# A decoder step of sparse attention and mLSTM: five hand-out times, two spacings, two orders

## The chip, the cores and the metric

The kernel runs on one core of one Trainium2 chip. The metric is device time in microseconds (us) for one execution of the whole step, given as the median of some runs. Five engines have queues of their own and run at the same time: TensorE (PE, matrix products), VectorE (DVE), ScalarE (ACT), GpSimd (POOL) and SyncE (SP). Transfers (DMAs) are started by instructions in the queue of an engine, here mostly SP, POOL and ACT.

## The reference, cut to what matters

One layer works on a prompt of 1024 tokens and on 8 decode tokens with 4096 cached positions each; together they are 1032 columns. In short:

```python
p = project(rmsnorm(x, norm_w), w_in, b_i, b_f)    # 14 column groups of one projection
# DSA heads, for each query:
s = einsum(relu(einsum(q_idx, k_idx)), w_idx) * IDX_SCALE      # 16 index heads of 64
_, idx = top_k(where(key_pos <= pos, s, -inf), 256)            # index search
att = softmax(q @ k[idx] * ATT_SCALE) @ v[idx]                 # 8 heads, 2 kv heads, 128 wide
# mLSTM heads, 4 of them: recurrence over the prompt with states C, n, m; one step for decode
h = num / maximum(abs(den), exp(-m_t))
a  = att * silu(z_att)
mo = rmsnorm(h) * ml_norm_w * sigmoid(o) * silu(z_ml)
y  = rmsnorm(x + concatenate([a, mo]) @ w_out) * final_norm_w
```

Outputs are y for prompt and decode, and the new k, v, index keys and mLSTM states. Everything is fp32. The decode tokens do the same search over their paged caches, and gather the 256 selected rows of k and v.

## The kernel before, in words

**Projection in tiles.** The 61 tiles of 128 output columns of w_in are worked off in program order; a tile is the unit in which all time is planned. fp32 products are made from a rounded high part (H) and the rest (L) of each operand: three matmuls, H·H, H·L and L·H. Tiles 0 to 20 (`proj`, L1591) hold the index queries and keys, k, v and q of attention. From tile `T_G` = 21 on `gate_stage()` works the other 40 tiles (mLSTM q, k, v, its gates o and z, and the gate of attention) as 20 column pairs of a Strassen-Winograd 2x2 form: 7 products for each pair, so 140 products of 48 matmuls (128x258, L1778). Stage 1 makes two of the seven for all pairs (products 0 to 39), stages 2, 3 and 4 one each (40 to 59, 60 to 79, 80 to 99), stage 5 the last two (100 to 139).

**Partial sums.** Between the stages a pair's partial sums lie in DRAM, in `spD`. `get` (L1795 to L1799) loads one, `combine` (L1874, on DVE) adds the product out of PE's banks, `put` (L1802) stores it. In stages 2 to 4 `ask(x, i)` calls `get` for pair i two products ahead; i = 0 and 1 are asked for before the stage. `get` stands in `issue_after(pace["put"])`: its load comes behind the last `put` store in SP's order. The partial goes into one of a few ring tiles (named `ev`, `rstd`, `xH` or `xL` in the rows, since these tiles reuse older memory). Weights come by L1763 on SP, their sums (`usD`) from POOL; the input's halves come by L1731 (`xL<-xsD`), and ACT (L1766) and DVE (L1767) split what has to be split.

**The jobs beside it.** Attention, index search and mLSTM are written as generators and handed out between the matmuls. A `Job(name, start, end, weight, gen, conditions)` stands in a `Lane`; lanes run their jobs one after the other. At each quarter tile the lane takes pieces up to a `yield`; a piece of weight w is charged w times the quarters left until `end`, over the weight that is left. So `end` and the number of yields set how densely a job is handed out. Lane 0 has gates, index (index scores L482 to L487 and search), att (attention of the prompt) and ml (mLSTM of the prompt). Lane 1 has prep, dscore and dsel (decode search), qrows (puts the decode queries into rows, L1287 and L992, and stores them as `qrowS`, L995), datt (decode attention; loads the rows back to all partitions, `qb`, L1305) and dml. Lane 2 makes the weight sums. att waits until datt is done; datt goes on only when index is done and tile 33.8 has been reached.

At the end of dsel SP stores the selected rows' numbers (`slotS<-rai`, L1186) and loads them in another layout (`idxs<-slotS`, L1187), one directly behind the other. att loads v blocks (`pP<-avS`, L603) and transposes them (L611). ml loads decay rows (`rb<-rowS`, L851) and q, k, v (L854), makes scores and transposes (L873 to L878), exponents on ACT, and products (L909, L915); its outputs go to `hS` (L948).

**The end.** The output projection begins with its last 264 columns (L2086) and goes on with the first 768 in Strassen form (L2153). Its input, the gated branch outputs, comes from loads of gate and branch on POOL (L1557, L1561), a product on DVE (L1568, L1569), the high part on ACT (L1576) and the low part on DVE (L1577). Weights come from SP as `wraw` (L265) and are split on ACT (L268) and DVE (L269).

A scheduler puts each engine's instructions into one fixed order when the program is built. `high_priority`, `pin` and `issue_after` steer it; adds that are listed in `late` are placed later with the rows that use them.

Of the kernel before, what the change touches and what calls it, by code (L numbers as in the profile page):

```python
# [42 lines left out]
T_AK = 9  # L43
T_AV = 11
T_AQ = 13
T_G = 21
# [131 lines left out]
def body(tc, A, stop=None):  # L178
# [27 lines left out]
    early = ExitStack()  # L206
# [15 lines left out]
    pace = {}  # L222
# [608 lines left out]
    def job_ml():  # L831
        gT = mlc["gT"]
        with tc.tile_pool(name="ml", bufs=2) as pm:
# [115 lines left out]

            steps = [(c, h0) for c in range(8) for h0 in (0, 2)]  # L950
            ld = [load(*steps[0])]
            for _ in range(3):
                yield 1
            ld.append(load(*steps[1]))
            yield 1
# [328 lines left out]
    def job_qrows():  # L1284
        with tc.tile_pool(name="qr", bufs=1, side="right") as pd:
            qc = pd.tile([128, NB, 8], F32, name="qc")
            V.tensor_copy(qc, dec[:, T_AQ:T_AQ + 8, :].rearrange("p j b -> p b j"))  # L1287
            yield 1
            rows(pd, qc.rearrange("p b j -> p (b j)"), qrowS, "jk")
            yield 1  # L1290

# [232 lines left out]
    def ix_weight(blocks):  # L1524
# [4 lines left out]
    groups = ((2, 3), (4, 5), (6, 7))  # L1529

    lanes = [Lane([Job("gates", 5, T_AK - 0.5, 14500, job_gates),
                   Job("index", T_AK + 1.5, 31.5, 6000 + sum(map(ix_weight, groups)), lambda: job_index(groups)),
                   Job("att", T_G + 18.2, 48.0, 2 * 2 * sum(2 * (1 + (i + 1) * 0.5) for i in range(8)) + 24, job_att, att_free),
                   Job("ml", T_G + 20, 56.4, 39, job_ml, lo_done)]),
             Lane([Job("prep", 3, T_AK + 1.8, 1 + 16 * 2, job_prep),
                   Job("dscore", T_AK + 2.4, 17.9, 56 + 128 + 2, job_dscore),
                   Job("dsel", T_AK, 27.2, 4000 + 31 * 1700 + 12000 + 16 * 2800 + 2000, job_dsel),
                   Job("qrows", T_G + 0.2, 28, 2, job_qrows),
                   Job("datt", T_G + 12.1, 38.0, 10000 + 8 * 8000 + 15000 + 5 * 2500 + 8000 + 8000 + 5000, job_datt),
                   Job("dml", T_G + 20, 55.5, 28000 + 16 * 2500 + 5000, job_dml, hi_done)]),  # L1540
             Lane([Job("sums", T_AK + 2.5, 33.0, 4 * NP + 2 * NS, job_usum)])]
# [132 lines left out]
    def gate_stage():  # L1674
# [22 lines left out]
        def ev():  # L1697
            return take("ev", outs)
# [92 lines left out]
        def flat(e):  # L1791
            return e.rearrange("p c t -> p (c t)")

        def get(x, i, e=None):
            with tc.high_priority():  # L1795
                e = ev() if e is None else e
                with tc.issue_after(pace["put"]):
                    SY.dma_start(flat(e), spD[x, i])
            return e  # L1799

# [83 lines left out]
        for i in range(0, NP, 2):  # L1884
# [4 lines left out]
            for y in range(2):  # L1889
                product(6, i + y, 2, both[y], False)  # L1890
                with tc.high_priority():
                    if X0[i + y][0] == "mk":
                        e = ev()
                        for c in range(2):
                            V.scalar_tensor_tensor(e[:, c], both[y][c], MK_SCALE, rs[:, c], OP.mult, OP.mult)
                    else:
                        e = combine(both[y], rs, OP.mult, ev())
# [13 lines left out]
        got = []  # L1911

        def ask(x, i):
            got.append(get(x, i))

        def asker(x, i):
            return (lambda: ask(x, i)) if i < NP else None
# [3 lines left out]
        for i in range(NP):  # L1921
            ps = two()
# [7 lines left out]
        for i in range(NP):  # L1930
            ps = two()
# [15 lines left out]
        for i in range(NP):  # L1947
            ps = two()
# [36 lines left out]
        for p, (z, i, y) in enumerate(order):  # L1985
# [9 lines left out]
            e, g = fetched.pop(p)  # L1995
# [121 lines left out]
    HB = NBK // 2  # L2117
    pt = ctx.enter_context(tc.tile_pool(name="pt", bufs=1, side="right"))
    ss = pt.tile([128, NBK, 8], F32, name="ss")
    yt = [[None] * 4 for _ in range(NBK)]  # L2120
# [86 lines left out]
    late = []  # L2207
# [31 lines left out]
    for n in range(2):  # L2239
        ps = banks3(n)  # L2240
# [29 lines left out]
    def add(y, p, x, op=OP.add):  # L2270
        return lambda: pin(V.tensor_tensor(y, p, x, op))  # L2271
# [6 lines left out]
    for n in range(2):  # L2278
        ps = banks3(n)
        for k in range(8):  # L2280
            with tc.high_priority():
                T_ = tsplit(wblock(1, n, k, *single(n, k)), None, n > 0)
            blocks(ps, k, sP2[k], T_, LOW)
            spread(2)
            j = 4 + k // 2 if n else k
            if k % 2 if n else k < 4:
                pairprep(j)
                if j < 5:
                    with tc.high_priority():
                        pairsub(j)  # L2290
        for b in LOW:
            late.append(add(yt[b][n], ps[b], yt[b + HB * n][n]))
        if not n:
            rows3(square, LOW, 0)
    spread(9)
# [58 lines left out]
    for n in range(2):  # L2354
        ps = banks3(n)
# [18 lines left out]
    for n in range(2):  # L2374
        ps = banks3(n)
# [26 lines left out]
    ps = banks3(0)  # L2402
# [10 lines left out]
    ps = banks3(1)  # L2413
# [83 lines left out]
```

## Time and profile before

| | |
|---|---|
| median of 3 runs | 1942.56 us (1938.98 to 1945.68) |
| the profiled execution | 1935.76 us |
| its span | 1934.0 us |
| PE busy | 1886.7 us, 98% |
| DVE busy | 1393.2 us, 72% |
| ACT busy | 913.9 us, 47% |
| POOL busy | 512.7 us, 27% |
| mean granted PE clock | 0.988 |

The span is the profiled execution from its first instruction to its last. Busy shares are means over the whole span. PE is busy nearly all of it; what it loses is read from the list of its waits, each with the line that waited and what released it, and from the granted clock in the stretch behind a wait. Times of rows count from the start of the span. A tile name in a row may be a reused one.

### The profile page before, as it was taken

The numbers are of one execution on the slowest core, as the hardware profiler recorded it, in microseconds if no ns is written. First come the engines' busy times: TensorE is split into PE (matmuls) and PEld (weight loads), VectorE is DVE, ScalarE is ACT, GpSimd is POOL, SyncE is SP. The second block draws the span as 40 slices with busy tenths as digits, with TensorE's granted clock in tenths as the row PEclk, the third lists the DMA queues.
The fourth block names the chain that finished last, engine by engine and source line by source line (L and its number), as shares of the span: only waits on it lengthen the run. The fifth ranks groups of instructions, "written<-read, shape, count | busy, mean of one in ns | idle before, by whom it ended". The sixth has DMA issues, their size and how long they took to land. (4 is left out here: it accounts for less than half of the span.)

```text
span 1934.0 us, 37287 instructions
## 1 busy us (share of the span) xinstructions
PE 1886.7 (98%) x13422; PEld 1817.4 (94%) x13422; DVE 1393.2 (72%) x3266; ACT 913.9 (47%) x1822; POOL 512.7 (27%) x600
## 2 busy tenths in 40 slices
PE   9999999999999999899999999999999989999997
PEld 9999999999999999899989999988999989987886
DVE  8554577467698886799655666547888866788776
ACT  8222254145534457532244564545566544454654
POOL 0699843320011001015211011001211341105541
PEclk9999999999999999999999999998999999999999
DMA  7577857666899778769986898556999968899797
GB/s 262 162 235 215 256 181 218 192 164 172 237 290 253 209 191 213 247 211 333 301 221 162 228 261 203 155 185 218 317 305 305 246 185 286 265 328 318 257 218 234
DMA packets 253701, 456.62 MB, mean 236 GB/s; under 512 B 38165, under 2 KB 113877, under 8 KB 249837
## 3 DMA queue, kind: packets, MB, share of 16 engines
q1 hardware_dynamic: 192445, 331.24, 52.5%
q0 software_dynamic: 27648, 102.34, 23.2%
q10 hardware_dynamic: 33424, 20.68, 3.6%
q8 instruction: 105, 1.72, 0.4%
q14 instruction: 79, 0.65, 0.1%
HBM read 363.72 MB, written 138.67 MB: 260 GB/s over the span
## 5 line engine op out<-in xcount | busy, mean ns | idle before, releaser
L1778 PE MATMUL pj<-xH 128*128 128x258 f32 x1920 | 547.9, 286 | 7.1 <-DVE rstd L1874 5.1
L1778 PE MATMUL pj<-xL,xH 128*128 128x258 f32 x1920 | 547.2, 285 | 0.0
L1778 PE MATMUL pj<-xH,xL 128*128 128x258 f32 x1920 | 546.4, 285 | 0.0
L1778 PEld LDWEIGHTS pj<-xH 128*128 128x128 f32 x1920 | 365.1, 190 | 9.8 <-DVE rstd L1874 5.3
L1778 PEld LDWEIGHTS pj<-xH,xL 128*128 128x128 f32 x1920 | 365.3, 190 | 1.7
L1778 PEld LDWEIGHTS pj<-xL,xH 128*128 128x128 f32 x1920 | 365.2, 190 | 1.6
L1591 PE MATMUL pj<-xH,wH 128*128 128x344 f32 (+1 forms) x816 | 264.8, 327 | 1.6 <-ACT xH L325 1.0
L1591 PE MATMUL pj<-xL,wH 128*128 128x344 f32 (+1 forms) x816 | 264.5, 324 | 0.1
L1591 PE MATMUL pj<-xH,wL 128*128 128x344 f32 (+1 forms) x816 | 264.5, 324 | 0.0
L269 DVE TENSOR_TENSOR wL<-wraw,wH 128x512 fp32r<-128x512 f32 (+2 forms) x151 | 118.8, 798 | 108.8 <-ACT wH L268 107.0
L268 ACT CAST wH<-wraw 128x512 fp32r<-128x512 f32 (+2 forms) x151 | 90.2, 608 | 204.8 <-PE pj L1591 130.0
L1591 PEld LDWEIGHTS pj<-xH,wH 128*128 128x128 f32 x816 | 153.2, 188 | 3.5 <-ACT xH L325 1.9
L1591 PEld LDWEIGHTS pj<-xL,wH 128*128 128x128 f32 x816 | 153.3, 188 | 0.6 <-DVE xL L326 0.3
L1591 PEld LDWEIGHTS pj<-xH,wL 128*128 128x128 f32 x816 | 153.3, 188 | 0.1
L1766 ACT CAST xH<-wH 128x1024 fp32r<-128x1024 f32 (+1 forms) x91 | 76.1, 836 | 131.0 <-PE pj L1778 73.3
L2153 PE MATMUL pj<-wH,sH 128*128 128x512 f32 x336 | 131.7, 392 | 4.1 <-DVE yt L2271 2.7
L2153 PE MATMUL pj<-wH,sL 128*128 128x512 f32 x336 | 131.5, 391 | 0.0
L1766 ACT CAST xH<-wL 128x1024 fp32r<-128x1024 f32 x91 | 76.1, 837 | 107.8 <-PE pj L1778 67.9
L2153 PE MATMUL pj<-wL,sH 128*128 128x512 f32 x336 | 123.2, 391 | 0.1
L484 ACT ACTIVATE rl<-bank 128x512 f32<-128x512 f32 (+2 forms) x160 | 79.1, 522 | 88.1 <-PE bank L482 45.5
L487 DVE SCALAR_TENSOR_TENSOR s<-rl,wiN,s 128x512 f32<-128x512 f32 (+2 forms) x150 | 106.6, 731 | 17.4 <-ACT rl L484 14.3
L1767 DVE TENSOR_TENSOR xL<-wH,xH 128x1024 fp32r<-128x1024 f32 (+1 forms) x91 | 87.1, 957 | 29.6 <-ACT xH L1766 29.3
(500 smaller groups left out, 4450.1 us busy)
## 6 DMA issues: line engine op xcount, KB each, us to landing
wraw<-in_wt_dram SPq DMA_DIRECT2D x144, 256.0 KB
usD<-in_wa_dram POOLq DMA_DIRECT2D x46, 512.0 KB, 7.8
wraw<-in_wa_dram SPq DMA_DIRECT2D x78, 256.0 KB
wraw<-in_wo_dram SPq DMA_DIRECT2D x64, 256.0 KB
usD<-in_wa_dram SPq DMA_DIRECT2D x26, 512.0 KB
wH<-in_wa_dram SPq DMA_DIRECT2D x25, 512.0 KB
wL<-in_wa_dram SPq DMA_DIRECT2D x24, 512.0 KB
spD<-ev SPq DMA_DIRECT2D x46, 258.0 KB
```

What stands on the lines that cost most here:

```text
L268: a = paced("act", SC.copy(H[:, s, :cols], raw[:, s, :cols]))
L269: return a, V.tensor_tensor(L[:, s, :cols], raw[:, s, :cols], H[:, s, :cols].bitcast(F32), OP.subtract)
L484: SC.activation(r[:, :cn], p[:, :cn], AF.Relu)
L487: v = V.scalar_tensor_tensor(s[:, c0:c0 + cn], r[:, :cn], wv, s[:, c0:c0 + cn], OP.mult, OP.add)
L1591: m = PE.matmul(ps[:cols, :cn], w_[:, k, :cols], x_[kk][:, c0:c0 + cn], start=(kk == ends[0] and z == 0), stop=(kk == ends[1] and z == 2))
L1766: paced("act", SC.copy(H[:, q], r))
L1767: paced("dve", V.tensor_tensor(L[:, q], r, H[:, q].bitcast(F32), OP.subtract))
L1778: PE.matmul(ps[c], w_[:, q, ks], x[y][:, c * CS:c * CS + CS], start=(first and q == 0 and k == 0 and z == 0), stop=(q == 1 and k == 3 and ...
L2153: PE.matmul(ps[b], S_[x][:, b * 128:b * 128 + 128], T_[y], start=(k == 0 and z == 0), stop=(k == 7 and z == 2))
```

## The change

Seven edits. Three ends in the table of jobs come sooner (index 31.5 to 28.2 tiles, att 48.0 to 47.3, ml 56.4 to 55.8), and att may start at tile 38.8 instead of 39.2. qrows ends later (28 to 29.4), and four yields instead of one stand between its copy `qc` and its rows. ml has five yields instead of three between its first and its second load. `get` has a new argument, and `ask` sets it for i = 0 and 1: those loads are no longer placed behind the last store of a partial. In the output projection, the adds of the second half of the columns are issued at once with high priority, and no longer put on the list `late`; the operands are the same. The diff:

```diff
--- before.py
+++ after.py
@@ -949,7 +949,7 @@
 
             steps = [(c, h0) for c in range(8) for h0 in (0, 2)]
             ld = [load(*steps[0])]
-            for _ in range(3):
+            for _ in range(5):
                 yield 1
             ld.append(load(*steps[1]))
             yield 1
@@ -1285,7 +1285,8 @@
         with tc.tile_pool(name="qr", bufs=1, side="right") as pd:
             qc = pd.tile([128, NB, 8], F32, name="qc")
             V.tensor_copy(qc, dec[:, T_AQ:T_AQ + 8, :].rearrange("p j b -> p b j"))
-            yield 1
+            for _ in range(4):
+                yield 1
             rows(pd, qc.rearrange("p b j -> p (b j)"), qrowS, "jk")
             yield 1
 
@@ -1529,13 +1530,13 @@
     groups = ((2, 3), (4, 5), (6, 7))
 
     lanes = [Lane([Job("gates", 5, T_AK - 0.5, 14500, job_gates),
-                   Job("index", T_AK + 1.5, 31.5, 6000 + sum(map(ix_weight, groups)), lambda: job_index(groups)),
-                   Job("att", T_G + 18.2, 48.0, 2 * 2 * sum(2 * (1 + (i + 1) * 0.5) for i in range(8)) + 24, job_att, att_free),
-                   Job("ml", T_G + 20, 56.4, 39, job_ml, lo_done)]),
+                   Job("index", T_AK + 1.5, 28.2, 6000 + sum(map(ix_weight, groups)), lambda: job_index(groups)),
+                   Job("att", T_G + 17.8, 47.3, 2 * 2 * sum(2 * (1 + (i + 1) * 0.5) for i in range(8)) + 24, job_att, att_free),
+                   Job("ml", T_G + 20, 55.8, 41, job_ml, lo_done)]),
              Lane([Job("prep", 3, T_AK + 1.8, 1 + 16 * 2, job_prep),
                    Job("dscore", T_AK + 2.4, 17.9, 56 + 128 + 2, job_dscore),
                    Job("dsel", T_AK, 27.2, 4000 + 31 * 1700 + 12000 + 16 * 2800 + 2000, job_dsel),
-                   Job("qrows", T_G + 0.2, 28, 2, job_qrows),
+                   Job("qrows", T_G + 0.2, 29.4, 5, job_qrows),
                    Job("datt", T_G + 12.1, 38.0, 10000 + 8 * 8000 + 15000 + 5 * 2500 + 8000 + 8000 + 5000, job_datt),
                    Job("dml", T_G + 20, 55.5, 28000 + 16 * 2500 + 5000, job_dml, hi_done)]),
              Lane([Job("sums", T_AK + 2.5, 33.0, 4 * NP + 2 * NS, job_usum)])]
@@ -1791,10 +1792,12 @@
         def flat(e):
             return e.rearrange("p c t -> p (c t)")
 
-        def get(x, i, e=None):
+        def get(x, i, e=None, early=False):
             with tc.high_priority():
                 e = ev() if e is None else e
-                with tc.issue_after(pace["put"]):
+                with ExitStack() as es:
+                    if not early:
+                        es.enter_context(tc.issue_after(pace["put"]))
                     SY.dma_start(flat(e), spD[x, i])
             return e
 
@@ -1911,7 +1914,7 @@
         got = []
 
         def ask(x, i):
-            got.append(get(x, i))
+            got.append(get(x, i, early=i < 2))
 
         def asker(x, i):
             return (lambda: ask(x, i)) if i < NP else None
@@ -2289,7 +2292,11 @@
                     with tc.high_priority():
                         pairsub(j)
         for b in LOW:
-            late.append(add(yt[b][n], ps[b], yt[b + HB * n][n]))
+            if n:
+                with tc.high_priority():
+                    add(yt[b][n], ps[b], yt[b + HB][n])()
+            else:
+                late.append(add(yt[b][n], ps[b], yt[b][n]))
         if not n:
             rows3(square, LOW, 0)
     spread(9)
```

The change moves instructions. Below are three places, with rows as the built program has them (line, operation, output and inputs, size); the line numbers of the changed kernel are up to 7 higher.

**SP, from the end of stage 1 on.** `rstd` is the tile that receives stage 2's first partial. Before:

```order
L1186 DMA slotS<-rai 128x16
L1187 DMA idxs<-slotS 128x16x1
L1802 DMA spD<-ev 128x516
L1731 DMA xL<-xsD 128x516
L1763 DMA wH<-usD 128x1024
L995 DMA qrowS<-jk 64x128
L1731 DMA xL<-xsD 128x516
L1802 DMA spD<-ev 128x516
L1798 DMA rstd<-spD 128x516
L1798 DMA ev<-spD 128x516
L1305 DMA qb<-qrowS 128x1024 x3
```

With the change:

```order
L1801 DMA rstd<-spD 128x516
L1764 DMA wH<-usD 128x1024
L1186 DMA slotS<-rai 128x16
L1187 DMA idxs<-slotS 128x16x1
L1805 DMA spD<-rstd 128x516
L1801 DMA ev<-spD 128x516
L1764 DMA wL<-usD 128x1024
L1732 DMA xL<-xsD 128x516
L995 DMA qrowS<-jk 64x128
L1764 DMA wH<-usD 128x512
L1805 DMA spD<-rstd 128x516
L1801 DMA ev<-spD 128x516
```

The load of the first partial stood behind the pair slotS and idxs and is now ahead of it. The three loads `qb` stood directly behind the first two loads of partials, while the low half of `rstd` was loaded five rows after them; now they stand two rows after the piece shown. Of the two halves of `rstd`, the other one is loaded far sooner, in the middle of stage 1. The pair slotS and idxs has moved by four weight loads (L1763, now L1764).

**PE, where ml begins.** `bank` is ml's output bank, `pj` that of the gate products. Before:

```order
L1778 MATMUL pj_5281<-xL,xH 128x258
L1778 MATMUL pj_5281<-xH,xL 128x258
L873 MATMUL bank<-qkv 128x128 x2
L875 MATMUL bank<-cst,qkv 128x128 x2
L878 MATMUL bank<-cst,qkv 128x128 x4
L909 MATMUL bank<-aH,dH 128x258
L915 MATMUL bank<-aH,ksH 128x258
L909 MATMUL bank<-aH,dH 128x258
```

With the change (48 matmuls of L1779 stand between the two pieces):

```order
L1779 MATMUL pj_5374<-xH 128x258
L1779 MATMUL pj_5374<-xL,xH 128x258
L1779 MATMUL pj_5374<-xH,xL 128x258
L873 MATMUL bank<-qkv 128x128 x2
L875 MATMUL bank<-cst,qkv 128x128 x2
L878 MATMUL bank<-cst,qkv 128x128 x4
L1779 MATMUL pj_5375<-xH 128x258
```

```order
L1779 MATMUL pj_5376<-xL,xH 128x258
L1779 MATMUL pj_5376<-xH,xL 128x258
L909 MATMUL bank<-aH,dH 128x258
L915 MATMUL bank<-aH,ksH 128x258
L909 MATMUL bank<-aH,dH 128x258
L915 MATMUL bank<-aH,ksH 128x258
```

The products L909 stood directly behind L873 to L878. Now a product of the gate stage stands between them. L873 itself is 4.5 products (of 48 matmuls) nearer to the program's start than it was, the first load of `rb` on SP 7 weight loads.

**DVE, where the gate stage ends.** `mx` and `mL` belong to the input of the output projection (L1569 and L1577, now L1570 and L1578), L1874 (now L1877) is the combine. Before, behind the last combine:

```order
L1577 TENSOR_TENSOR mL_18608<-mx,mH_18607 128x264
L1829 SCALAR_TENSOR_TENSOR rstd<-rstd 128x516
L1830 SCALAR_TENSOR_TENSOR rstd<-xL,rstd 128x516
L1829 SCALAR_TENSOR_TENSOR ev<-ev 128x516
L1830 SCALAR_TENSOR_TENSOR ev<-xL,ev 128x516
L300 MEMSET rr 128x16
L1569 SCALAR_TENSOR_TENSOR mx<-mH_18793,nw,mL_18794 128x264
L1577 TENSOR_TENSOR mL_18794<-mx,mH_18793 128x264
L269 TENSOR_TENSOR wL<-wraw,wH 128x512 x3
L1569 SCALAR_TENSOR_TENSOR mx<-mH_18858,nw,mL_18859 128x264
L1577 TENSOR_TENSOR mL_18859<-mx,mH_18858 128x264
```

With the change, around the last combine:

```order
L1570 SCALAR_TENSOR_TENSOR mx<-mH_18793,nw,mL_18794 128x264
L1877 TENSOR_TENSOR rstd<-pj_5375,xH 128x258
L1578 TENSOR_TENSOR mL_18608<-mx,mH_18607 128x264
L1578 TENSOR_TENSOR mL_18794<-mx,mH_18793 128x264
L1832 SCALAR_TENSOR_TENSOR rstd<-rstd 128x516
L1833 SCALAR_TENSOR_TENSOR rstd<-xL,rstd 128x516
L1877 TENSOR_TENSOR ev<-pj_5376,xH 128x258
L1570 SCALAR_TENSOR_TENSOR mx<-mH_18858,nw,mL_18859 128x264
L1877 TENSOR_TENSOR ev<-bank,xH 128x258
L1578 TENSOR_TENSOR mL_18859<-mx,mH_18858 128x264
L1832 SCALAR_TENSOR_TENSOR ev<-ev 128x516
L269 TENSOR_TENSOR wL<-wraw,wH 128x512
```

Before, the last two products `mx` (18793 and 18858) stood behind the last combine and behind its gates (L1829, L1830), the last of them at the end of the piece. Now 18793 and 18858 stand ahead of the last combine, and 18858's low part directly behind it. The loads of their operands on POOL stand sooner in the same way, and ml's last matmul (L945) on PE is 4.7 products nearer to the start. From the output projection on, the orders of PE, DVE, ACT and SP are the same in both programs.

## The prediction

> **What bounds the kernel now.** I read the page first, then PE's waits, then busy time by stretch, then each engine's rows around each wait. All times are microseconds (us).
>
> ```profile
> span 1934.0 us, 37287 instructions
> PE 1886.7 (98%) x13422; PEld 1817.4 (94%) x13422; DVE 1393.2 (72%) x3266; ACT 913.9 (47%) x1822; POOL 512.7 (27%) x600
> ```
>
> TensorE (PE) is busy for 1886.7 of 1934.0. The change takes no matmul away, so it can win only what PE loses: idle time, and matmuls that run at a lower clock. PE's waits:
>
> ```profile
> PE bank L2086 <- ACT mH L1576: 6.0, 3, 2.9
> PE bank L873 <- DMA rb<-rowS: 5.2, 1, 5.2
> PE pj L1778 <- DVE rstd L1874: 5.1, 1, 5.1
> PE bank L611 <- DMA pP<-avS: 3.0, 1, 3.0
> PE pj L2153 <- DVE yt L2271: 2.7, 1, 2.7
> PE bank L992 <- DVE qc L1287: 2.4, 1, 2.4
> PE bank L909 <- ACT aH L895: 1.9, 1, 1.9
> PE bank L2086 <- ACT wH L268: 1.5, 1, 1.5
> ...
> PE bank L611 <- DMA spD<-ev: 0.9, 1, 0.9
> ```
>
> Columns: total, times, longest. A few single waits hold nearly all of it. Each has a second price, which the next view shows: stretches that start where such a wait ends (the sixth row takes in a wait itself, the last is an undisturbed stretch). After the two lengths stand the busy times, with counts, of PE, weight loads, DVE, ACT and POOL, then the granted clock, DMA share and GB/s.
>
> ```profile
> 761.50:767.00 5.50, 5.50 (x34) 5.50 (x35) 3.46 (x13) 3.56 (x7) 0.00 (x0) 0.69 0.64 92
> 791.70:798.00 6.30, 6.30 (x33) 6.30 (x34) 4.10 (x13) 2.84 (x5) 0.00 (x0) 0.59 0.68 244
> 971.60:978.00 6.40, 6.38 (x31) 6.38 (x32) 2.42 (x5) 2.46 (x4) 0.51 (x1) 0.52 1.08 339
> 1307.50:1310.00 2.50, 2.46 (x10) 2.10 (x10) 0.42 (x1) 0.27 (x1) 0.00 (x0) 0.50 0.32 125
> 1311.90:1316.50 4.60, 4.60 (x25) 4.60 (x26) 3.46 (x12) 1.59 (x5) 0.39 (x2) 0.59 0.44 133
> 1586.40:1598.00 11.60, 3.88 (x11) 2.15 (x10) 6.90 (x14) 3.74 (x8) 1.09 (x2) 0.60 0.54 165
> 1598.00:1603.00 5.00, 4.93 (x23) 4.71 (x24) 3.61 (x6) 2.19 (x5) 0.00 (x0) 0.56 0.78 261
> 1761.80:1767.00 5.20, 5.15 (x16) 4.12 (x17) 5.20 (x9) 2.41 (x6) 3.32 (x3) 0.67 0.90 288
> 600.00:700.00 100.00, 100.00 (x749) 95.52 (x748) 89.11 (x198) 45.72 (x76) 8.31 (x12) 1.00 0.78 207
> ```
>
> After a wait the granted clock is 0.5 to 0.7 for some six us. I price it as busy time times (1 minus the clock) and name the places:
> - **A**, decode query rows (L992): 2.4 idle + 5.50 × 0.31 = 1.7, so 4.1.
> - **B**, first combine of stage 2: 5.1 + 6.30 × 0.41 = 2.6, so 7.7.
> - **C**, start of the attention job (L611): 3.0 + 0.9 + 6.38 × 0.48 = 3.1, so 7.0.
> - **D**, start of the mLSTM job: 5.2 + 1.9 + 2.46 × 0.50 = 1.2 + 4.60 × 0.41 = 1.9, so 10.2.
> - **E**, start of the output projection. These two rows show one matmul taking 0.12 when nothing is waited for:
>
> ```profile
> 1581.86 0.29 PE L2086 MATMUL bank<-mH,wH 128*128 128x264 f32 x1
> 1581.98 0.29 PE L2086 MATMUL bank<-mL,wH 128*128 128x264 f32 x1
> ```
>
>   So 11 matmuls in 11.6 us are 1.3 of work and 10.3 lost; 4.93 × 0.44 = 2.2 more: 12.5.
> - **F**, in the output projection (L2153): 2.7 + 5.15 × 0.33 = 1.7, so 4.4.
>
> Together 45.9. Of that 28.9 is idle time (2.4 + 5.1 + 3.9 + 7.1 + 7.7 + 2.7), out of the 47.3 for which PE is not busy; the rest is lowered clock, which counts as busy.
>
> The Trainium skill ("TensorE: Matmul & The Clock Gate", section "HAM oscillation — how this bites in real kernels") gives gaps over about 3.4 us as what lowers the clock. A and F do not agree: gaps of 2.4 and 2.7 are followed by 0.69 and 0.67. By that rule a remaining gap of some 2 us at A would cost 1.7 less than I charge.
>
> **The change part by part.** Columns in the rows below: start, length, queue or engine, line, operation; in brackets idle time and what ended it.
>
> *A and B: qrows in more pieces, and first partials without the order behind a store.*
>
> ```profile
> 754.65 0.32 SPq L1186 DMA_DIRECT2D slotS<-rai  x1
> 761.08 0.37 SPq L1187 DMA_DIRECT2D idxs<-slotS  x1
> 761.15 0.22 DVE L1287 COPY qc<-dec 128x64 f32<-128x64 f32 x1 [5.62 <-DMA slotS<-rai]
> 771.52 1.28 SPq L1305 DMA_DIRECT2D qb<-qrowS  x3
> 781.92 0.32 SPq L1798 DMA_DIRECT2D rstd<-spD  x1
> 791.20 0.76 DVE L1874 TENSOR_TENSOR rstd<-pj,rstd 128x258 f32<-128x258 f32 x2 [0.28 <-DMA rstd<-spD]
> ```
>
> B: the partial sum that stage 2 needs first is issued at 781.92 and combined at 791.20, 9.3 later. Just ahead of it on SP's queue stand three loads of 128x1024 floats, 512 KB each, 1.5 MB in all. In the changed order the two first partials stand ahead of slotS, and the three qb loads come after them, behind the stores and loads of two further partials. PE waited from 786.6 on; the load can lose 5.1 of its 9.3 and still be on time, and with no 1.5 MB ahead of it 4.2 is ample: at the 244 GB/s of the stretch from 791.7 its 258 KB are 1.1. The load of the other rstd half moves far forward, into stage 1. Taken: all of B, 7.7; bounds 0 (the load is slow for another reason) and 7.7.
>
> A: the wait is the 6.4 from slotS (8 KB) to idxs, during which SP issues nothing and DVE waits 5.6. Both move some four weight loads later, into stage 2, and are not shortened. Behind slotS now queue idxs, the store and load of the next partial and the next weights; behind qc the first combines. Stage 2 rotates three banks, so DVE's wait of 5.6 is covered for about half of a 48-matmul product, 48 × 0.12 = 5.8, i.e. 2.9. What is left is some 2 to 3 idle at L992 or at a bank, with its clock price: 4. Taken: 0 gained; bounds +4.1 (covered) and −7.7 (a stall as at B).
>
> The Trainium skill ("DMA: Bandwidth & Descriptors", section "Anatomy of one DMA — SWDGE (gpsimd) path") puts a small transfer at about 2.0 us. The row has 6.4 on SP's queue, so I keep 6.4. By the 2.0 (an estimate from that page) the wait would fit into the covered 2.9, and A's 4.1 would be won as well.
>
> *C: att handed out sooner, after an index search that ends sooner.*
>
> ```profile
> 959.53 0.32 SPq L603 DMA_DIRECT2D pP<-avS  x1
> 961.74 0.49 SPq L603 DMA_DIRECT2D pP<-avS  x1
> ```
>
> L611 ended its wait near 971.6, ten us after the second issue, in a stretch whose DMA share is 1.08. Counted in products of 48 matmuls along PE's order and in weight loads along SP's, L611 stood before at 70.1 to 70.6 with its loads at 74.5 and 75.0; SP runs four or five loads ahead there, so there was no lead. In the change they stand at 64.5 and 66.0: three products, some 17 us, more than the ten. Taken: all 7.0; bounds 0 (the queues are full there whatever the place) and 7.0.
>
> *D: ml's yields, and its sooner end.*
>
> ```profile
> 1298.67 0.43 SPq L851 DMA_DIRECT2D rb<-rowS  x1
> 1307.54 1.19 PE L873 MATMUL bank<-qkv 128*128 128x128 f32 x4 [5.16 <-DMA rb<-rowS]
> ```
>
> The load is issued 8.9 before the matmul starts, 3.7 before PE wants it. In the change the first loads stand about two products ahead of L873, 11.5. And between L873 to L878 and L909 stand 48 matmuls, 5.8 of work, which cover the 1.9 of ACT's exponent chain. Taken: 10.2; bounds 5 (only one of the two waits goes, about half) and 10.2.
>
> *E: ml's end at 55.8 instead of 56.4.*
>
> ```profile
> 1560.96 0.37 ACTq L948 DMA_DIRECT2D hS<-hT  x1
> 1564.08 0.54 POOL L1557 DMA_DIRECT2D mL<-gateS  x1 [7.81 <-ACT xH L1766]
> 1572.71 23.02 SPq L265 DMA_DIRECT2D wraw<-in_wo_dram  x9
> 1584.41 0.42 DVE L1874 TENSOR_TENSOR ev<-bank,xH 128x258 f32<-128x258 f32 x1
> 1594.32 0.49 DVE L1569 SCALAR_TENSOR_TENSOR mx<-mH,nw,mL 128x264 f32<-128x264 f32 x1
> ```
>
> After its last hidden-state store POOL starts two dozen loads one behind the other, from 1564.08 on, DVE makes the mixes from them, and the last mix comes at 1594.32, 9.9 after the last combine. In the change ml's last matmul stands 4.7 products (27 us) sooner, those loads stand between earlier stores on POOL, and the last mix stands on DVE directly at the last combine. What can remain is the weights: nine loads of w_out occupy SP for 23.0, and the view of waits has 1.5 for them. Remaining: 1.5 + the 2.2 of clock + 0.3 = 4. Taken: 8.5; bounds 0 (weights set the start) and 12.5.
>
> *F and the late adds.* From the output projection on, the order of DVE around L2271 is the same row for row, so this edit moves nothing: 0, cover not needed.
>
> *What the earlier work displaces.* The index's remaining work goes into 17.7/21 of the time. Its largest groups on DVE between 300 and 760:
>
> ```profile
> L487 DVE SCALAR_TENSOR_TENSOR s<-rl,wiN,s 128x512 f32<-128x512 f32 (+2 forms) x120 | 74.8, 648 | 13.9 <-ACT rl L484 13.5
> L557 DVE TENSOR_SCALAR_CACHE_REDUCE gt<-s,sm 128x384 bf16<-128x384 f32 (+1 forms) x32 | 23.8, 744 | 0.8
> ```
>
> 98.6 of 460 is 21%; times 21/17.7 it is 4 points more: 600 to 700 goes from 89% to 93%. That is under full, but each time a backlog outlasts DVE's lead over PE a new stall appears. All jobs get new neighbours, so I charge one new stall of B's size, 7.7; bounds 0 and two, 15.4.
>
> **Sum:** 7.7 + 0 + 7.0 + 10.2 + 8.5 + 0 = 33.4, less 7.7, is 25.7. The profiled execution took 1935.76 (span 1934.0), so 1910.1 on its scale. The median of the runs shown is 1942.56, 6.8 above it: **1917** on theirs.
>
> **The rivals.**
> 1. *Half.* The output projection waits for w_out's weights, so E stays whole, and two new stalls appear. For: 23.0 us of weight issues just before it. Against: the waits put 6.0 on the mixes and 1.5 on weights. 33.4 − 8.5 − 15.4 = 9.5: 1933.
> 2. *The stalls only move.* The hand-out in tiles gives every job another neighbour, and what was late at B, C and D is late elsewhere. For: A's wait does just that. Against: at B, C and D the new leads (11.5 and 17) are longer than the waits. 1942, give or take 4.
> 3. *Slower: DVE is the bound in stage 1.* Place: products 0 to 39, PE waiting for operand splits and combines. For: 89% before, 93% after, and above that in clusters, since score matmuls bunch up at products 4 to 6 (20 in one against 14). Against: without any of this PE lost nothing in 500 to 700, with 89%. Each stall costs 7.7; it decides from five on (33.4 / 7.7 = 4.3); with six, 46.2 − 33.4 = +12.8: 1955.
>
> **How the numbers follow.** Likeliest case 0.63, half 0.19, only moved 0.08, slower 0.10. The likeliest case's own range is 1903 (no new stall, A gone too: 33.4 + 4.1 = 37.5, and 2 for the run-to-run spread) to 1927 (two new stalls: 18.0 gained, and 2.4 for the spread). The range 1903 to 1937 takes in the half case. A change within 0.3%, 5.8 us, can't be told from none. Faster needs below 1936.7: the first case and most of the second, 0.63 + 0.17 = 0.80. Same: 0.02 + 0.07 = 0.09; slower: 0.10 + 0.01 = 0.11.
>
> **What would show it.** Right: among PE's waits L873 on rb, rstd at stage 2's start, and L611 on avS are gone or below 1; the mixes no longer end L2086's waits; a wait of 2 to 3 stays at qc or moves to a combine of stage 2; F is there with some 2.7. Wrong: stage 1 shows a row of new waits on L1767's splits or L1874's combines with the clock below 1 behind them (rival 3); w_out's weights end 5 or more (rival 1); or PE's busy time stays at 98% with the same total lost under other names (rival 2).

## The result and the profile after

The changed kernel takes 1914.12 us (median of 4 runs, 1911.52 to 1916.13), the kernel before 1944.12 in the runs beside it (1938.98 to 1948.62). The ratio is 0.9846 with a 95% interval of 0.9817 to 0.9874: 1.5% faster, some 30 us. In a second group of runs the ratio was 0.9872 (0.9848 to 0.9896). The profiled executions differ by less, 1935.76 and 1914.8, since the profiled execution of before was one of its fastest. One of the ten executions of e3 (below) took 3732 us; it counts as slow and is left out of e3's ratio.

The page of the changed kernel (span 1913.0 us), its busy times:

```profile
PE 1880.4 (98%) x13422; PEld 1809.8 (95%) x13422; DVE 1399.1 (73%) x3266; ACT 916.8 (48%) x1822; POOL 515.3 (27%) x600
```

PE's waits in the changed kernel (total, times, longest):

```profile
PE bank L482 <- ACT rl L484: 6.5, 9, 2.8
PE bank L1041 <- DMA kp<-in_cik_dram,idx: 3.3, 1, 3.3
PE pj L2156 <- DVE yt L2274: 2.8, 1, 2.8
PE pj L1779 <- ACT mH L1577: 1.7, 2, 1.4
PE bank L909 <- POOL st L931: 1.5, 1, 1.5
PE bank L2089 <- ACT wH L268: 1.4, 1, 1.4
...
PE bank L701 <- ACT ptH L696: 0.9, 1, 0.9
```

The waits of A, B, C and D are no longer in the list at all, and of E 1.4 is left. F (L2156 on yt) is there with 2.8. The 1.5 at L909 waits for POOL (`st`), not for the exponents as at D. New are waits of the index scores (L482), together 6.5, a longer one of the decode scores (L1041), 3.3 after 1.3, and 1.7 at the gate products that end on the high part of the output projection's input (`mH`), which ACT now makes beside them.

How the places stand now, in the rows of the changed kernel, first A and B:

```profile
787.44 0.32 SPq L1801 DMA_DIRECT2D rstd<-spD  x1
791.58 0.43 DVE L1877 TENSOR_TENSOR rstd<-pj,rstd 128x258 f32<-128x258 f32 x1
792.32 0.32 SPq L1186 DMA_DIRECT2D slotS<-rai  x1
795.44 0.37 SPq L1187 DMA_DIRECT2D idxs<-slotS  x1
795.45 0.22 DVE L1287 COPY qc<-dec 128x64 f32<-128x64 f32 x1 [1.49 <-DMA slotS<-rai]
803.74 1.27 SPq L1306 DMA_DIRECT2D qb<-qrowS  x3
```

The first partial is issued at 787.44 and combined 4.1 us later, not 9.3: the three large qb loads come 16 us behind it. The pair slotS and idxs holds SP for 3.1 and not 6.4, and DVE waits 1.5 and not 5.6 for it; PE does not notice. C, D and E:

```profile
914.19 0.79 SPq L603 DMA_DIRECT2D pP<-avS  x2
931.87 1.03 PE L611 MATMUL bank<-cst,pP 128*128 128x128 f32 x8
...
1254.71 0.42 SPq L851 DMA_DIRECT2D rb<-rowS  x1
1271.54 0.60 PE L873 MATMUL bank<-qkv 128*128 128x128 f32 x4
...
1513.98 0.38 PE L945 MATMUL bank<-cst,hm 128*128 128x128 f32 x2
...
1570.09 0.49 DVE L1570 SCALAR_TENSOR_TENSOR mx<-mH,nw,mL 128x264 f32<-128x264 f32 x1 [0.63 <-DMA mH<-hS]
1570.50 0.42 DVE L1877 TENSOR_TENSOR ev<-bank,xH 128x258 f32<-128x258 f32 x1
```

Each pair gives a lead: 17.7 us from the v loads to L611 and 16.8 from the first rb load to L873. ml's last matmul is at 1514 (before 1555), and the last mix starts ahead of the last combine.

**Where the time went, by stretch.** To compare kernels whose orders differ I took, for each profiled execution, the time of a stretch on PE and subtracted, for each matmul in it, the time from the start of one matmul of that shape to the start of the next (the median in before's profile, for instance 0.12 for 128x258). What is left is loss, idle and lowered clock together, in us. A row's level depends on these medians, so what counts is the difference between two columns; the sums differ as the spans do (before to change 21.0). Stretches are counted in products of the gate stage; the columns e1 to e8 are the experiments below.

```
                  before  e2    e3    e4    e5    e6    e1   change  e7    e8
ahead of prod. 0   11.7  17.3  16.5  16.9  17.5  18.5  19.1  19.4  20.2  26.1
0-35 (stage 1)      1.4   1.2   1.6   1.2   1.0   4.3   4.6   6.8  10.3   4.7
35-50 (A, B)       11.7  10.2  11.3  11.3   4.5  -0.1   0.3  -0.1   3.4   4.6
50-62              -0.2   0.6   0.6   0.4  -0.1  -0.2   2.4   2.4  -0.2  10.7
62-80 (C)          11.2  12.1  14.0  11.1  12.8   7.6   0.3   3.9   9.2   1.5
80-96               0.3   0.3   0.3   0.3   0.2   0.3   1.3   0.5   1.9   0.5
96-108 (D)         13.1  11.2   7.2  15.1   5.5  19.9   1.6   2.2   2.0   0.4
108-139.5           0.0   3.6   3.4   9.5   2.6   1.3   8.4   2.3   0.4  -0.1
139.5-end (E, F)   28.4  30.4  36.4  20.3  28.9  28.6  20.6  19.3  20.5  19.5
sum                77.6  86.9  91.1  86.1  73.0  80.2  58.3  56.6  67.7  67.8
```

From before to the change A and B give back 11.8, D 10.9, E 9.1. C gives back 4.7, counted with the row 50-62, into which small matmuls of the decode attention move. The index search, handed out more densely, costs 7.7 ahead of product 0 and 5.4 in stage 1, and 2.3 are lost in 108 to 139.5. Four kernels with the search as it was (e2 to e5) show that before's own profile is unusually low ahead of product 0, by 5.3 (mean 17.0 against 11.7); against those the search costs 2.4 there and 5.5 in stage 1. This makes up 5 of the 9 us by which the medians lie further apart (30) than the profiles (21).

### The profile page after: what moved, and what is told of

It reads as the page before. It is cut to its first block, busy times and chain, and to the rows that moved or that the text cites. A ratio compares the mean times of both kernels' runs of the same rounds, so it can differ in the third digit from the quotient of the medians.

```text
span 1913.0 us, 37341 instructions
## 1 busy us (share of the span) xinstructions
PE 1880.4 (98%) x13422; PEld 1809.8 (95%) x13422; DVE 1399.1 (73%) x3266; ACT 916.8 (48%) x1822; POOL 515.3 (27%) x600
## 5 line engine op out<-in xcount | busy, mean ns | idle before, releaser
L1779 PE MATMUL pj<-xH 128*128 128x258 f32 x1920 | 546.8, 285 | 1.7 <-ACT mH L1577 1.7
L1779 PE MATMUL pj<-xL,xH 128*128 128x258 f32 x1920 | 545.6, 284 | 0.0
L1779 PE MATMUL pj<-xH,xL 128*128 128x258 f32 x1920 | 545.3, 285 | 0.0
L1779 PEld LDWEIGHTS pj<-xH 128*128 128x128 f32 x1920 | 363.6, 190 | 4.1 <-ACT mH L1577 2.1
L1779 PEld LDWEIGHTS pj<-xH,xL 128*128 128x128 f32 x1920 | 363.6, 190 | 2.0 <-issue 0.4
L1779 PEld LDWEIGHTS pj<-xL,xH 128*128 128x128 f32 x1920 | 363.9, 190 | 1.5
L2156 PE MATMUL pj<-wH,sH 128*128 128x512 f32 x336 | 131.7, 392 | 3.7 <-DVE yt L2274 2.8
L2156 PE MATMUL pj<-wH,sL 128*128 128x512 f32 x336 | 131.5, 391 | 0.0
L1767 ACT CAST xH<-wH 128x1024 fp32r<-128x1024 f32 x91 | 76.0, 835 | 108.8 <-PE pj L1779 61.9
L2156 PE MATMUL pj<-wL,sH 128*128 128x512 f32 x336 | 123.3, 392 | 0.3 <-DVE wL L2145 0.3
L1768 DVE TENSOR_TENSOR xL<-wH,xH 128x1024 fp32r<-128x1024 f32 x91 | 87.0, 956 | 20.2 <-ACT xH L1767 18.6
```

The lines of the kernel that those rows point to most:

```text
L1767: paced("act", SC.copy(H[:, q], r))
L1768: paced("dve", V.tensor_tensor(L[:, q], r, H[:, q].bitcast(F32), OP.subtract))
L1779: PE.matmul(ps[c], w_[:, q, ks], x[y][:, c * CS:c * CS + CS], start=(first and q == 0 and k == 0 and z == 0), stop=(q == 1 and k == 3 and ...
L2156: PE.matmul(ps[b], S_[x][:, b * 128:b * 128 + 128], T_[y], start=(k == 0 and z == 0), stop=(k == 7 and z == 2))
```

## The experiments

Two of the seven edits can be told from the built orders alone. With the qrows edit taken out of the change, or put alone into the kernel before, every engine's order is the same row for row as without it; so also with the late adds. These two edits move nothing, and they were not run. That leaves the index search's end, att's start and end, ml's end and yields, and the early partials. Two theories stood against each other: ONE CAUSE (the index search's end alone moves what A to E hang on) and EACH ITS OWN (the prediction's working, edit by edit).

**e1: the index search's end alone.**

```diff
-Job("index", T_AK + 1.5, 31.5, ...      (kernel before)
+Job("index", T_AK + 1.5, 28.2, ...
```

> The kernel before with one edit, the index search's end at 28.2 instead of 31.5. Two theories. ONE CAUSE: the end of the index search alone moves what the waits A to E hang on; in the built order of this kernel slotS, qc and the qb loads stand where the whole change has them, behind the first partials of stage 2, the v loads of att have the change's lead, ml's first product stands one product behind its scores, and ml's last matmul 2.9 of the 4.7 products sooner. So A, B, C are gone, D mostly, E at least half: 18 to 26 us faster, 1918 to 1926. EACH ITS OWN (the prediction's working): the index's end and att's serve C alone, so only 7.0 goes: about 1937, with A, B, D and E still among the waits.

Measured: 1916.45, ratio 0.9849 (0.9823 to 0.9876): the change's whole gain from one number (28 us by the medians, where ONE CAUSE said 18 to 26). Its PE waits:

```profile
PE bank L945 <- ACT hm L937: 4.5, 1, 4.5
PE bank L482 <- ACT rl L484: 4.4, 4, 1.5
```

A to E are gone, as in the change. ONE CAUSE holds, EACH ITS OWN falls. A wait of 4.5 in ml (L945) is here and not in the change; by the stretches above it is made up for by smaller losses in stage 1 and at C, so that ml's edits, att's and the early partials win nothing in sum. Att's edit was not run alone.

**e2: the early partials alone.** `get(x, i, early=i < 2)` as in the diff, in the kernel before.

> The kernel before with one edit, the first two partials of stages 2 to 4 loaded without the order behind a store. EACH ITS OWN: B goes, 7.7 faster, about 1936. ONE CAUSE: the built order shows one of the first loads far sooner, but the load that B waited for still stands behind the three qb loads, so B stays at about 5 idle and the time within 4 us of before.

Measured: 1945.48, ratio 1.0003 (0.998 to 1.0025). Its waits still hold the combines of stages 2 and 3 (3.9 is the longest, at stage 2's start 3.8):

```profile
PE pj L1778 <- DVE rstd L1876: 8.2, 3, 3.9
```

The edit does nothing for B: of the two tiles' loads only one comes sooner, and B waited for the other.

**e3: ml's two edits alone.**

```diff
-for _ in range(3):       ... 56.4, 39, job_ml      (kernel before)
+for _ in range(5):       ... 55.8, 41, job_ml
```

> The kernel before with both edits of ml (five yields and weight 41, end 55.8). EACH ITS OWN: D and E go, 18.7 faster, about 1925. ONE CAUSE: in the built order the first loads of rb stand 104 products' worth of weights into SP's queue with the scores at 103.5 on PE (before 105), and ml's last matmul stands at 135.6 (before 135.4), so E stays whole and D loses only its second wait, some 2 to 4: about 1941.

Measured: 1948.23, ratio 1.0008 (0.999 to 1.0026): nothing, where even ONE CAUSE said 3. D's stretch fell from 13.1 to 7.2, as the second of D's waits was spaced out; the one on the output projection's input rose (L2086 on mH: 7.2 in 6 waits, before 6.0 in 3). In the order ml ended no sooner.

**e4: the whole change with the index search's end back.**

```diff
-Job("index", T_AK + 1.5, 28.2, ...      (kernel changed)
+Job("index", T_AK + 1.5, 31.5, ...
```

> The whole change with the index search's end back at 31.5. EACH ITS OWN: C is back, the rest of the gain stays, 1921 or so. ONE CAUSE: A, B and C are back in the waits, D's first wait too (ml's scores stand at 103.5 again), ml's last matmul is 1.9 products sooner than before, which takes some of E: 1934 to 1944.

Measured: 1948.28, ratio 1.0025 (1.0012 to 1.0038). Six edits of seven give no gain; they are a little slower, and slower than ONE CAUSE said. Its waits:

```profile
PE pj L1779 <- DVE rstd L1877: 8.8, 2, 5.3
PE pj L1779 <- DVE ev L1877: 7.6, 2, 7.0
...
PE bank L611 <- issue: 3.2, 1, 3.2
...
PE bank L873 <- issue: 3.0, 1, 3.0
...
PE bank L992 <- DVE qc L1287: 2.3, 1, 2.3
```

A, B, C and D are all back (at two of these places the profile shows no releaser, only "issue"), with a new one of 7.0 ahead of the output projection, which takes E's place. So the end of the index search is needed and, by e1, enough. The next two runs ask by what path it acts.

**e5: B's order without the index search.** The decode selection comes later, and with it slotS and qb.

```diff
-Job("dsel", T_AK, 27.2, ...   Job("qrows", T_G + 0.2, 28, 2, ...      (kernel before)
+Job("dsel", T_AK, 28.8, ...   Job("qrows", T_G + 0.2, 29.6, 2, ...
```

> The kernel before, with only the decode selection handed out later (dsel's end 27.2 to 28.8, qrows' end 28 to 29.6); index, att and ml as before. In the built order slotS and the qb loads then stand at and behind the partials that stage 2 needs first, as in the whole change, and nothing else is moved much (L611 at 69.4 products, v loads half a weight load behind it; ml as before). Theory PLACE ON SP (A and B are a matter of where those small and large loads stand against the first partials, whatever moves them): B below 1 idle, A at most 2, C, D and E as before: 7 to 12 faster, 1933 to 1937. Rival INDEX CROWDING (B and A come from the index search's own load on DVE in stage 2): B stays, within 4 of before.

Measured: 1925.29, ratio 0.9892 (0.9865 to 0.9919). The waits:

```profile
PE bank L873 <- ACT d L867: 3.4, 1, 3.4
PE bank L611 <- DMA pP<-avS: 3.4, 1, 3.4
...
PE bank L992 <- DVE im L559: 2.5, 1, 2.5
PE pj L1778 <- DVE rstd L1874: 2.0, 2, 1.8
```

```profile
785.23 0.97 SPq L1798 DMA_DIRECT2D rstd<-spD  x1
790.31 0.43 DVE L1874 TENSOR_TENSOR rstd<-pj,rstd 128x258 f32<-128x258 f32 x1 [2.19 <-DMA rstd<-spD]
```

The later of the two loads of `rstd` is combined 5.1 after its issue, with qb behind it, where before took 9.3 with qb ahead. The stall at stage 2's start is gone (the 1.8 here is at 936, in stage 3), C and E are there. A is there too, but L992 waits for another DVE result (im). PLACE ON SP holds for B: once qb stands behind the first partials, B goes, whoever moves it. But the gain, some 20 by the medians, is larger than B: in the profile D's stretch fell as well, from 13.1 to 5.5, and this profiled execution (1931.25) was the slowest of its four. Why D fell is not shown, so the excess over the 7 to 12 is not explained.

**e6: the index search sooner, but decode attention as late as before.**

```diff
-Job("index", T_AK + 1.5, 31.5, ...   Job("datt", T_G + 12.1, 38.0, ...      (kernel before)
+Job("index", T_AK + 1.5, 28.2, ...   Job("datt", T_G + 12.1, 41.5, ...
```

> The index search's end at 28.2 in the kernel before, as in the run with that edit alone, and datt's end at 41.5 instead of 38.0, so that att and ml come as late as before (L611 at 74.0 products, its v loads half a weight load behind it; ml's scores at 103.5, the rb loads at 105; ml's last matmul at 135.5). Theory LATER IS LATE (C, D and E hang on when datt ends, and the index search only lets it end sooner): A and B gone, C, D and E back: 10 to 14 faster than before, 1931 to 1935. Rival ROOM (with the index search out of stage 2, DVE and the queues have room whatever the hour): at least C and D stay away, 1920 to 1926.

Measured: 1943.64, ratio 0.9997 (0.9979 to 1.0015). The waits:

```profile
PE bank L873 <- DMA rb<-rowS: 10.1, 1, 10.1
PE bank L2086 <- ACT mH L1576: 5.2, 5, 2.7
PE bank L482 <- ACT rl L484: 4.6, 6, 1.3
PE bank L648 <- ACT qH L631: 3.5, 1, 3.5
```

A and B stay away (-0.1 in their stretch). D is back at half as much again (19.9 after 13.1), E is back whole (28.6 after 28.4), and C's place is taken by a wait of 3.5 at L648. LATER IS LATE holds: ending sooner the search lets decode attention, att and ml come sooner, and it is this that C, D and E hang on. I expected 10 to 14 of gain from A and B; the larger D and the search's own waits took it.

What moves is DVE's work. Two rows of each kernel, first before, then the change; after the lengths stand busy PE, weight loads and DVE:

```profile
760.00:900.00 140.00, 133.41 (x1080) 133.24 (x1081) 115.47 (x248) 58.36 (x89) 27.22 (x22) 0.96 0.79 247
900.00:960.00 60.00, 59.01 (x501) 56.92 (x500) 44.31 (x80) 16.57 (x26) 21.88 (x21) 1.00 1.02 313
```

```profile
760.00:900.00 140.00, 140.00 (x1171) 139.52 (x1171) 126.50 (x245) 45.95 (x68) 50.00 (x36) 1.00 0.90 284
900.00:960.00 60.00, 60.00 (x487) 57.12 (x486) 34.91 (x84) 23.30 (x44) 7.06 (x8) 1.00 0.90 255
```

In 760 to 900 DVE does 11 us more and in 900 to 960 9 less: jobs queued behind the search are done sooner, so att's loads are issued at 914 and not at 960.

**e7 and e8: how much sooner?** The whole change with the end of the search at 29.2 and at 27.2.

```diff
-Job("index", T_AK + 1.5, 28.2, ...      (kernel changed)
+Job("index", T_AK + 1.5, 29.2, ...      (e7; 27.2 in e8)
```

> The whole change with the index search's end at 29.2 instead of 28.2. By the built order: qb behind the partials as in the change, so A and B stay away; the v loads at 68 against L611 at 66.6 (in the change 63 against 64.5), the rb loads at 101.5 against 100.0 (98 against 99). LEAD theory (a wait is there where the loads stand behind their matmul in these counts): C is back with 3 or more idle and D's first wait too: 8 to 14 slower than the change, 1922 to 1928. Rival GRADUAL (the gain goes with how early the search ends, a third of the way back): about a third of 30 lost, 1924 as well, but with a part of every wait A to E back.

> The whole change with the index search's end at 27.2. The leads are those of the change (v loads 62.5 against 64.5, rb 98 against 99). LEAD theory: nothing more to win, C to E stay away; the search itself is denser, so its own waits (L482 on the ReLU) grow from 6.5 to about 8 to 10: 1914 to 1918. GRADUAL: another 6 to 9 faster, 1905 to 1908. If DVE is full in stage 1: new waits on splits or combines there, 1920 or more.

Measured: 1926.32, ratio 0.9904 (0.9879 to 0.9929), and 1927.79, ratio 0.992 (0.989 to 0.9949). Both are some 12 us slower than the change; their runs (1925.27 to 1927.87 and 1926.37 to 1933.65) do not touch the change's. Of e7, then of e8:

```profile
PE bank L482 <- ACT rl L484: 7.1, 2, 6.4
PE bank L1041 <- DMA kp<-in_cik_dram,idx: 6.2, 1, 6.2
...
PE pj L1779 <- DVE rstd L1877: 2.3, 1, 2.3
PE bank L611 <- issue: 2.2, 1, 2.2
PE bank L648 <- ACT qH L631: 2.2, 1, 2.2
```

```profile
PE bank L482 <- ACT rl L484: 7.4, 12, 1.8
...
PE pj L1779 <- issue: 4.6, 5, 3.5
PE pj L1779 <- DVE ev L1877: 2.6, 2, 2.0
```

GRADUAL falls with e8: the time does not go with how early the search ends. By e7 alone it could stand, since parts of several waits are back there. LEAD is half right for e7: C is back in part (2.2 and 2.2; 9.0 lost in 50 to 80 against 6.3), D is not (2.0 against 2.2). What it did not say: 4.3 of the 11 us between the profiles are lost ahead of product 35, with a single wait of 6.4 in the search and a longer one on kp, and 3.5 in 35 to 50, where a combine at stage 2's start waits 2.3 again. In e8 A, C, D and E stay away, but the stretch ahead of product 0 loses 6.7 more than in the change. Stage 1 is no slower (its first 35 products take 234.7, in the change 237.5). Most is lost in products 35 to 62, 13.0 more, at new waits on combines (L1877) and on "issue", the longest 3.5 at 873; what those waited for is not shown. So of the three values 28.2 is the best, with a collision of another kind on each side, and not a point on a slope.

**e9 to e12: the change again, and what is left in it.** e9 is the change itself, run beside the next three. The wait of L1041 is there in all the kernels above. The third gather of index keys (kp) stands on POOL behind weight sums that wait for their own loads:

```diff
             fetch(1)
+            fetch(2)
...
-                    fetch(b * 4 + c + 2)      (ahead of a block's matmuls)
+                    fetch(b * 4 + c + 3)      (behind the matmuls that free the tile)
```

e10 has this edit; e11 also does the two sums of one more weight block in the output projection on POOL instead of DVE (`k > 2` for `k > 3`); e12 of two more blocks (`k > 1`).

> The whole change itself, beside the three runs below on the same chip: 1914, the measure for them. Its profile should again have none of the waits A to E, the ReLU waits (L482) near 6 and the wait on kp (L1041) at 3 to 5.

> The whole change, with the gathers of the decode search's index keys (kp) issued as soon as a tile is free: the third one stands ahead of POOL's weight sums instead of behind them. Nothing but four rows of POOL's order changes. Theory: the wait of L1041 on kp, 3.3 to 6.2 in all the profiles so far but one, goes, with the lowered clock that sometimes follows: 3 to 6 faster than the change, 1908 to 1911. Rival: DMA is what is slow there and the weight sums behind the gather then come late: within 2 of the change.

> As the run before, and in the output projection the two sums of one more weight block on POOL instead of DVE. Theory: at F DVE is full (no idle row between 1728 and 1745 but 1.3), so two operations of 0.6 less let the adds come 1.2 sooner: F's 2.8 falls to 1.5 or so, 1 to 2 faster than the run before. Rival: POOL's sums take 1.3 to 1.5 each and come late: new waits of L2156, slower by 1 to 4.

> As the run before, with the sums of two more weight blocks on POOL. Theory: F is gone (2.4 less on DVE), 3 to 5 faster than with kp alone. Rival: four sums in a row on POOL, 5.6 in all, come late for PE: slower than with one block.

Measured, all beside a median of 1939.07 for before:

```
      median us (runs)              ratio to before
e9    1912.74 (1908.06-1920.20)     0.9872 (0.9848-0.9896)
e10   1904.83 (1904.44-1912.31)     0.9837 (0.9814-0.9859)
e11   1913.19 (1909.88-1917.41)     0.9867 (0.9845-0.9889)
e12   1909.91 (1907.52-1913.86)     0.9856 (0.9835-0.9877)
```

e9 has none of the waits A to E, 7.8 at L482 and 3.3 on kp. POOL's rows in e10, and its wait of L1041:

```profile
289.86 1.19 POOL L1020 DMA_INDIRECT kp<-in_cik_dram,idx  x1 [0.30 <-issue]
291.06 1.86 POOL L1488 DMA_DIRECT2D usD<-in_wa_dram  x2
```

```profile
PE bank L1041 <- DMA kp<-in_cik_dram,idx: 0.7, 1, 0.7
```

The third gather now leaves at 289.86, ahead of the sums (in the change at 300.42), and the wait falls from 3.3 to 0.7; in e11 and e12 it is not in the list at all. e10 has the lowest median of all and is below both kernels, though its interval overlaps e9's. Some of its 8 us may be chance: e11 and e12, with the same gathers, are at +0.5 and -2.8 to e9. With the sums taken at nothing, a mean over the three gives 3.4 for the gathers, within the expected 3 to 6. The stretch ahead of product 0 agrees: it loses 15.7, 16.1 and 16.9 in e10 to e12 against 20.9 in e9. In stage 1, where the orders are the same, e11 loses 11.5, and e10 and e12 4.7 and 5.1.

The sums on POOL did not help. F is 3.3 in e11, where 1.5 was expected, and falls to 1.1 in e12, but there 2.5 come at another place of L2156 (on the weight split wH). Whether F can be had for less stays open.

## Why the prediction was right, and where it was not

The time (1917 forecast, 1914 measured), its direction and the list of waits that would go were right. The reasons for them were in part wrong.

- **What bounds the kernel.** Right: PE's busy time changed by only 6 us (1886.7 to 1880.4), and the gain is the waits at A to E with their clock, less what the denser search costs.
- **B.** The size fits: 7.7 of the 11.8 that A and B give together. The step that failed is "first partials without the order behind a store" as its cause. e2 has that edit and keeps B; e1 has not and loses it. What counts is the other sentence of that step, that the qb loads stand ahead of the partial (e5), and it is the index search that moves them. The reading of before's row was too narrow as well: the combine waited only 0.28 for its own load. DVE came to it late, since a split ahead of it waited for ACT, and ACT for a weight load (wL) that SP issued directly behind the three qb loads. So the partial was not all that was late behind them:

```profile
788.01 1.04 ACT L1766 CAST xH<-wL 128x1024 fp32r<-128x1024 f32 x1 [2.15 <-DMA wL<-usD]
789.09 1.23 DVE L1767 TENSOR_TENSOR xL<-wL,xH 128x1024 fp32r<-128x1024 f32 x1 [1.44 <-ACT xH L1766]
```

- **A.** Mis-sized: 0 taken, about 4 gained (what 11.8 leaves beside B). "qrows in more pieces" changes no order, and no wait of 2 to 3 stays at qc or moves to a combine. The hold of 6.4 was taken over from before's row; in its new place it was 3.1. The two-microsecond figure that the Trainium skill ("DMA: Bandwidth & Descriptors", section "Anatomy of one DMA — SWDGE (gpsimd) path") gives for a small transfer was the better estimate of the outcome. That is partly luck, as the section is on transfers that POOL issues and this pair is issued by SP: other runs show the same pair at 8.2 (e5, from 776.61 to 784.77) and 2.3 (e1, from 790.59 to 792.90).
- **C.** 7.0 taken, 4.7 found in 50 to 80. The wait at L611 is gone, with the lead that the orders showed; a wait of 0.9 with a lowered clock at L701 came in its place. In e1 the same stretch gains 8.3.
- **D.** 10.2 taken, 10.9 found. The lead is seen in the rows, 16.8 where 11.5 was said. The step "ml's yields" is not what makes it: e3 takes 6 of D and wins nothing in the end, e1 takes 11.5.
- **E.** 8.5 taken, 9.1 found, 1.4 of wait on wH left where 1.5 was said. ml's own end alone did nothing (e3).
- **F.** Right: 2.7 before, 2.8 after.
- **What the earlier work displaces.** The size, 7.7, is what the runs give against typical executions (2.4 + 5.5 = 7.9), and less than the 13.1 against before's own profile. That it fits is luck, since it was charged as one stall of B's size by a reason that failed: DVE's busy share between 500 and 700 did not rise by 4 points, it fell (86.3 to 82.8, and 89.1 to 86.6). It rose earlier: between 300 and 500 from 134.9 us to 143.9, 4.5 points. The waits are at L482. The longest, 2.8, starts at 550.9 with ACT's ReLU tile lent to a bias store that was still on its way:

```profile
546.24 0.59 SPq L576 DMA_DIRECT2D biasS<-rl  x1
553.03 0.98 ACT L484 ACTIVATE rl<-bank 128x512 f32<-128x512 f32 x2 [4.23 <-DMA biasS<-rl]
```

- **The rivals.** *Half*: w_out's weights held the start for 1.4 to 2.4 in e9 to e12 and the change, not for 5. *Only moved*: it fits e4 and e6, not the change. *DVE the bound in stage 1*: neither at 28.2 nor at 27.2 (e8), where stage 1 loses less than in the change; in e8 waits on combines appear in stage 2, with the other gains still larger.

The sum came out right because the places and their prices were read from before's rows, and because the built order showed that the places would go. Some of it is luck: A came out 4.1 larger, C 2.3 smaller, the 2.3 lost in 108 to 139.5 were not foreseen, and these nearly cancel. That seven edits stood in the diff did not mean that each had its share.

## What to carry to other kernels

- When a change has several edits, compare the built order with each edit alone before giving a gain to any of them. Here two edits move no instruction, four move some and gain nothing in sum, and one number does it all.
- A wait is often made far from where it shows: a job that ends sooner on the busiest side engine brings forward what is queued behind it, and that gives later loads their lead. A hand-out time is worth trying on both sides of its value: 1 tile to either side cost some 12 us here.
- Here a small store whose result is loaded back on the same queue held up the load, and what stood behind it, for 2.3 to 8.2 us, and an urgent load behind three large ones was used 9.3 us after its issue, with them behind it after 5.1 (e5) or 4.1 (the change). Look at what stands around the late load, not only at when it is issued.

## What the runs showed that was not expected

**The clock.** In the fourteen profiles there are 96 single waits of 0.7 us or more on PE (none of that length in the 20 us before, none in the 8 after; the wait at each kernel's very start is not counted). The granted clock in the 8 us that follow:

```
length of the wait    waits   with a lowered clock
0.7 to 2.0            47      6
2.0 to 3.4            26      19
3.4 to 3.7            7       6
3.7 and more          16      16
```

The lowered value is most often 0.79. That is half speed for 3.4 of the 8 us, so 1.7 us lost per wait, whether it was 2.3 or 4.2 long. These rows of the changed kernel, behind the wait of 2.8 at L482, show it, the first a part of the second:

```profile
554.20:557.50 3.30, 3.30 (x15) 3.20 (x15) 3.10 (x7) 2.11 (x4) 0.00 (x0) 0.50 0.03 12
553.60:561.60 8.00, 7.92 (x43) 7.58 (x44) 7.09 (x12) 5.10 (x11) 1.31 (x2) 0.79 0.18 64
```

The Trainium skill ("TensorE: Matmul & The Clock Gate", section "What's actually happening") describes a free-running window of about 3.4 us, idle for one of which lowers the clock. The price of 3.4 us at half speed agrees with that window. As a bound on the wait it does not agree: 19 of 26 waits of 2.0 to 3.4 were followed by a lowered clock, and one of 3.61 (e2, at 977) was not. For a forecast, a wait of 2 to 3.4 us costs itself plus 0.7 × 1.7 by these counts, and one above 3.7 itself plus 1.4 or more within the 8 us (in all 16).

**Spread.** Before's runs lie between 1932.86 and 1954.02 over all groups, 1.1% apart, with no order changed. The stretch ahead of product 0 in its profile differs by 5 us from that of kernels with nearly the same order. A sum of losses from one profile can be off by that much, and the comparison against the median carries it.
